# Two transformer layers on one core: the issue order of a list-scheduling planner, after key shifts drawn from a kept list of seeds

## The chip, the cores and the metric

The kernel runs on one core of a Trainium2 chip, as one launch. The core has five engines that each work through a queue of instructions in a fixed order: PE (matrix multiply), DVE (vector), ACT (scalar and activation functions), POOL (a second, slower vector engine) and SP, which here only issues transfers. An instruction starts when the one ahead of it on its engine lets it and when the data and buffers that it needs are there; semaphores carry this between engines. The metric is the device time of the launch in microseconds (us). Three runs of the kernel before took 1334.98, 1337.83 and 1337.9 us; the median is 1337.83 us.

## The reference

One batch of 1024 latent tokens (a grid of 16 rows by 64 columns) and 256 context tokens, both 1024 wide, goes through two layers. Layer A is grouped-query attention with 16 query heads on 4 key and value heads; layer B is neighbourhood attention with 16 heads, a window of 8 by 16 grid positions, a learned bias and the context tokens as extra keys. Each layer has its own modulation vectors, a gate branch and an output projection. What is computed, cut to its core:

```python
for i in range(2):
    sh_x, sc_x, g_x = split(silu(c) @ w_mod[i] + b_mod[i])        # and the same with c_ctx for the context
    hx = rms_norm(x, norm_g[i]) * (1 + sc_x) + sh_x
    hc = rms_norm(ctx, norm_g[i]) * (1 + sc_c) + sh_c
    # layer 0: q, k, v, z = hx @ w_in; q, k = rope(rms_norm(q)), rope(rms_norm(k)); keys and values of ctx go ahead
    #          p = softmax(q k^T / 8 over 1280 keys);  yx = ((p v) * silu(z)) @ w_out; the same for ctx with its own keys
    # layer 1: q, k, v, z = hx @ w_in;  p = softmax([q k_window^T / 8 + rpb, q k_ctx^T / 8])
    #          yx = ((p_window v_window + p_ctx v_ctx) * silu(z)) @ w_out
    x = x + g_x * yx
    # layer 0 alone: ctx = ctx + g_c * yc
return rms_norm(x, final_norm_g)
```

All of it is in 32-bit floats in the reference.

## The kernel before

**Precision.** Products run in 16-bit floats. An operand that needs more is split into a high part (a cast) and a low part (what the cast left over, times a power of two), and a product is then two or three matmuls. The splits are the work of ACT (casts), DVE and POOL (differences).

**Layer A** goes through the heads in pairs, eight of them. For each pair PE makes the projections (tile `pa`, line 1029), DVE, ACT and POOL norm and rotate them, and a pass of score products (`pm`, lines 1063 and 1069) gives the row maxima. Then come the score products themselves. Most heads use products that stand with keys on the partitions (`st`, lines 1255 and 1256); ACT takes two exponentials (`ph` in 16 bits, line 1240; `pf` in 32 bits, line 1242), POOL takes their difference (`pl`, line 1125, in two halves), and PE multiplies with the values (`pv`, lines 1131 to 1133). Some heads use products with queries on the partitions (`qs`, lines 1181 and 1182); their probabilities `qpp` are turned by a transfer (line 1200, a transpose that SP issues) before PE uses them (`qpv`, lines 1206 and 1208). The output projection of the layer is `poa` (line 1353), with a DVE product (`tm`, line 1357) and a POOL sum into `x` (line 1358) behind each tile. The modulation vectors of the second layer come from `pmg` (line 636), which reads weights `wg` that a transfer brings.

**Layer B** first norms `x` again (an ACT square at line 668 into `hrb`, DVE at 672 and 673, casts at 684), and makes its projections in a form with fewer products: sums of weight blocks `wtb` (POOL, lines 1429 to 1431, from loaded blocks `wsb`) are cast to `wb` (high part on ACT at line 1433, low part on DVE at 1434) and used at lines 1512 (`pwq`) and 1560 (`pwv`), with the context's products at 1522 (`pbc`) and 1572 (`pvc`). Attention then runs by head pair: scores `bsn` against the window and `bsc` against the context (lines 1593 and 1594), bias and row maximum on DVE (line 1612) with a bias table `tb` that POOL makes (lines 1412 to 1414), exponentials on ACT (1630 to 1633), the split on POOL (1125 again), a transposing transfer `bpht` (line 1636), and the products with the values (`bpv`, lines 1641 to 1644). The output weights `wsob` are loaded (line 1298), scaled (line 1300, POOL) and split (`wob`, line 726 on DVE); the output projection is `pob` (line 1734), then a sum and the last norm.

**What sets the order.** The Python code records all instructions once, with the stages interleaved by a coarse plan. Then class `Planner` reads them back: `graph` finds the dependencies and the buffers that each instruction opens, `cost` gives each an estimated time, and `schedule` plays the five engines forward. Each engine keeps a heap of the instructions whose inputs are there, and takes the one with the smallest key. `deadlines` works back from a finished schedule to a due time for each instruction. The key of a PE instruction is its start in the schedule before, and that of any other is its due time. `refine(5, …)` repeats this five times and keeps the order with the smallest modelled end. `apply` then fixes each engine's order by a dependency from every instruction to its next one. Names in the listings further down end in numbers that tell buffers and instances apart (`x19` is a tile of `x`, `poa00` the first output projection tile, `qpp1130` a probability tile).

Of the kernel before, what the change touches and what calls it, by code (L numbers as in the profile page):

```python
# [37 lines left out]
BEV, BLAG = 8, 4  # L38
BP0, BP1 = 0, 0.95
PFB, PHB, PTB = 5, 4, 6  # L40


class Planner:
# [437 lines left out]
        end = max(done)  # L481
        return [min(v, end) for v in due]

    def refine(self, rounds, margin, deadline):

        best = (max(self.done), self.order)
        self.log = [best[0]]
        for _ in range(rounds):
            due = self.deadlines(deadline)
            key = [s if e == "PE" else v for s, e, v in zip(self.start, self.eng, due)]  # L490
            best = min(best, (self.schedule(key.__getitem__, margin=margin), self.order), key=lambda b: b[0])
            self.log.append(max(self.done))
        self.order = best[1]

    def apply(self):
        info = mybir.DependencyInfo(mybir.DependencyClass.NoSync, mybir.DependencyReason.DATA)
# [1343 lines left out]
```

## Time and profile before

The profiled execution took 1334.24 us, 3.59 us under the median of the runs. Its span, from the first to the last record, is 1332.5 us; 1.74 us lie around it.

| what | value |
|---|---|
| runs, us | 1334.98, 1337.83, 1337.9 (median 1337.83) |
| profiled execution, us | 1334.24 (span 1332.5, mean clock of PE 0.995) |
| PE busy | 1300.4 us, 98% of the span, 14948 matmuls |
| DVE busy | 1071.4 us, 80% |
| ACT busy | 966.0 us, 72% |
| POOL busy | 888.1 us, 67% |
| idle time of PE | 32.1 us |
| chain that ended last | PE 74%, DVE 12%, ACT 6%, DMA 4%, issue 2%, POOL 1% |

The table's last row follows the work that ended last back to the start, at each step to what released it. In the views below, a row of a timeline gives the start and the length in us, the engine, the line of the code, the operation, the tile written and the tiles read, and at its end in brackets how long the engine stood idle ahead of it and which instruction released it. Ends of matmuls are modelled, so that each looks longer than its share of the engine: the starts tell the pace. A row of a table by stretch gives the stretch, its length, then for PE, weight loads, DVE, ACT and POOL the busy time with the number of instructions, and last the granted clock of PE, the share of the DMA engines and GB/s.

### The profile page before, as it was taken

The numbers are of one execution on the slowest core, as the hardware profiler recorded it, in microseconds if no ns is written. First come the engines' busy times: TensorE is split into PE (matmuls) and PEld (weight loads), VectorE is DVE, ScalarE is ACT, GpSimd is POOL, SyncE is SP. The second block draws the span as 40 slices with busy tenths as digits, with TensorE's granted clock in tenths as the row PEclk, the third lists the DMA queues.
The fourth block names the chain that finished last, engine by engine and source line by source line (L and its number), as shares of the span: only waits on it lengthen the run. The fifth ranks groups of instructions, "written<-read, shape, count | busy, mean of one in ns | idle before, by whom it ended". The sixth has DMA issues, their size and how long they took to land.

```text
span 1332.5 us, 38402 instructions
## 1 busy us (share of the span) xinstructions
PE 1300.4 (98%) x14948; PEld 923.5 (69%) x14948; DVE 1071.4 (80%) x2451; ACT 966.0 (72%) x2076; POOL 888.1 (67%) x1214
## 2 busy tenths in 40 slices
PE   9999999999999999999999989999999999999997
PEld 4457777777777777776654448779687786968553
DVE  5897787888889786769628997888888898989475
ACT  4653888878988877698742456878879788887453
POOL 2322777766877767687876456687766867877452
PEclk9999999999999999999999999999999999999999
DMA  9825467886777323244318962587766888979962
GB/s 368 245 69 121 96 136 140 158 158 137 150 150 143 69 67 83 59 123 105 102 36 211 224 144 81 120 155 152 154 135 148 149 146 149 169 159 208 294 150 107
DMA packets 391791, 192.17 MB, mean 144 GB/s; under 512 B 350072, under 2 KB 356408, under 8 KB 391608
## 3 DMA queue, kind: packets, MB, share of 16 engines
q1 hardware_dynamic: 391032, 189.67, 64.0%
q8 instruction: 117, 1.92, 0.6%
q14 instruction: 66, 0.54, 0.1%
q10 hardware_dynamic: 576, 0.03, 0.0%
HBM read 91.54 MB, written 15.75 MB: 81 GB/s over the span
## 4 chain that ended last, share of the span: by engine, by line
PE 74%; DVE 12%; ACT 6%; DMA 4%; issue 2%; POOL 1%; SPq 0%; DVEq 0%; POOLq 0%; ACTq 0%
PE pa L1029 13%; PE poa L1353 7%; PE pob L1734 6%; PE st L1256 3%; PE st L1255 3%; PE pm L1063 3%; PE pv L1132 2%; PE pv L1133 2%; PE pv L1131 2%; DVE wb L1434 1%; PE pkv L882 1%; DMA qpp<-qpp 1%; PE pbc L1522 1%; PE qpv L1206 1%; PE qs L1181 1%
## 5 line engine op out<-in xcount | busy, mean ns | idle before, releaser
L1125 POOL TENSOR_TENSOR pl<-pf,ph 128x256 f16<-128x256 f32 x400 | 271.7, 703 | 67.8 <-ACT pf L1242 44.0
L1125 POOL TENSOR_TENSOR bph<-bpf,bph 128x256 f16<-128x256 f32 (+1 forms) x224 | 184.8, 851 | 105.5 <-ACT bpf L1632 84.3
L1029 PE MATMUL pa<-wa,x 128*128 128x256 f16 x1536 | 226.0, 273 | 0.5 <-DVE mrow L638 0.4
L1240 ACT ACTIVATE ph<-st 128x512 f16<-128x512 f32 x240 | 144.2, 606 | 60.3 <-PE st L1256 56.9
L1560 PEld LDWEIGHTS <-hx 128*128 128x128 f16 x2688 | 157.6, 98 | 11.5 <-issue 3.6
L1029 PEld LDWEIGHTS <-x 128*128 128x128 f16 x1536 | 140.1, 98 | 35.0 <-issue 2.0
L1242 ACT ACTIVATE pf<-st 128x512 f32<-128x512 f32 x240 | 144.7, 608 | 1.7 <-DVE pl L1122 1.3
L1064 DVE TENSOR_REDUCE mxp<-pm 128x1 f32<-128x512 f32 x192 | 127.3, 685 | 16.3 <-PE pm L1063 14.2
L1131 PE MATMUL pv<-v,ph 128*128 128x65 f16 x960 | 126.0, 193 | 0.0
L1132 PE MATMUL pv<-v,ph 128*128 128x64 f16 x960 | 125.9, 195 | 0.0
L1125 POOL TENSOR_TENSOR qpp<-qpf,qpp 128x256 f16<-128x256 f32 (+1 forms) x158 | 92.9, 611 | 48.0 <-ACT qpf L1198 31.5
L1133 PE MATMUL pv<-v,pl 128*128 128x65 f16 x960 | 123.8, 192 | 0.0
L1512 PEld LDWEIGHTS <-wb 128*128 128x128 f16 x672 | 63.1, 98 | 69.3 <-issue 4.8
L1630 ACT ACTIVATE bph<-bpf,bnx 128x384 f16<-128x384 f32 (+1 forms) x128 | 70.6, 584 | 53.3 <-DVE bnx L1622 39.9
L1131 PEld LDWEIGHTS <-ph 128*128 128x128 f16 x960 | 91.1, 97 | 22.5 <-issue 0.2
L1132 PEld LDWEIGHTS <-ph 128*128 128x128 f16 x960 | 90.8, 97 | 15.3
L1133 PEld LDWEIGHTS <-pl 128*128 128x128 f16 x960 | 91.4, 99 | 11.3 <-POOL pl L1125 1.3
L1255 PE MATMUL st<-q,k 128*128 128x512 f16 x240 | 90.9, 379 | 1.4 <-ACT pf L1242 1.3
L1256 PE MATMUL st<-q,k 65*128 65x512 f16 x240 | 91.2, 383 | 0.0
L1353 PE MATMUL poa<-woa,oa 128*128 128x512 f16 x384 | 90.2, 379 | 0.0
L1734 PE MATMUL pob<-wob,obf 128*128 128x512 f16 x336 | 80.0, 379 | 0.0
L1429 POOL TENSOR_TENSOR wtb<-wsb 128x256 f32<-128x256 f32 x64 | 58.7, 918 | 31.9 <-DVE wb L1434 7.5
(480 smaller groups left out, 4035.4 us busy)
## 6 DMA issues: line engine op xcount, KB each, us to landing
wg<-in_w_mb SPq DMA_DIRECT2D x32, 512.0 KB
wsb<-in_b_wp SPq DMA_DIRECT2D x64, 256.0 KB
wm<-in_w_m SPq DMA_DIRECT2D x16, 512.0 KB
wsa<-in_a_wq SPq DMA_DIRECT2D x32, 256.0 KB
xstage<-in_x SPq DMA_DIRECT2D x8, 512.0 KB
wsoa<-in_a_w_out SPq DMA_DIRECT2D x16, 256.0 KB
x<-in_x SPq DMA_DIRECT2D x8, 512.0 KB
x_d<-x SPq DMA_DIRECT2D x8, 512.0 KB
```

What stands on the lines that cost most here:

```text
L1029: T.matmul(ps[:, :, i, :], hA(a, kt, t), wt[w][:, kt, :], start=n == 0, stop=n == 3 * KT - 1)
L1125: G.tensor_tensor(lo[:, c], p32[:, c], hi[:, c], op=ALU.subtract)
L1131: T.matmul(pv[:, t, :], hi[:, c], v[:, 0:65], start=first and t == 0, stop=False)
L1132: T.matmul(pv[:, t, 0:HD], hi[:, c], v[:, 65:129], start=False, stop=False)
L1133: T.matmul(pv[:, t, :], lo[:, c], v[:, 0:65], start=False, stop=last and t == n - 1)
L1240: S.activation(ph, st, AF.Exp)
L1242: S.activation(p32, st, AF.Exp)
L1255: T.matmul(so, k1[:, g, kc], q1[:, :, i, :], start=True, stop=False)
L1256: T.matmul(so, k2[0:65, g, kc], q2[0:65, :, i, :], start=False, stop=True)
L1353: T.matmul(ps, lhs(a, kt), w[b][:, kt, :], start=n == 0, stop=n == 3 * KT - 1)
L1560: T.matmul(ps[:, t * P:(t + 1) * P], hx[a][:, t, blk, kt], wt[j][:, s_, w, kt], start=first and t == 0 and m == 0, stop=last and t == 3 an ...
L1734: T.matmul(ps, ob[kt][:, t, a], wout["b"][hf][b][:, kt, :], start=n == 0, stop=n == 3 * len(kts) - 1)
```

## The change

`refine(5, …)` is replaced by `settle(2, seeds, …)`. Two rounds of due times and scheduling are run as before, without choosing among them. Then, for each of about 330 numbers in the kept list `NUDGE`, a random generator with that number as its seed draws a time between 0 and 1330 us, a width (2, 10 or 40 us), a spread (0.3, 1 or 4 us) and a subset of the five engines; the keys of the instructions of these engines that lie in that stretch of time are shifted by normal draws of that spread, one draw for each output tile on each engine. One last call of `schedule` with the shifted keys gives the order. The instructions, their operands and buffers stay as they were; so do the dependencies that `graph` finds, and only the order on each engine is another. Lines of the new kernel stand 37 further down than those of the kernel before (1353 is 1390).

```diff
+NUDGE = (
+    "688836 233264 233275 606456 325627 589506 889935 702195 564303 420536 171248 386454 369054 445142 567028 "
...
+)
...
-    def refine(self, rounds, margin, deadline):
-
-        best = (max(self.done), self.order)
-        self.log = [best[0]]
+    def settle(self, rounds, seeds, margin, deadline):
+
         for _ in range(rounds):
             due = self.deadlines(deadline)
             key = [s if e == "PE" else v for s, e, v in zip(self.start, self.eng, due)]
-            best = min(best, (self.schedule(key.__getitem__, margin=margin), self.order), key=lambda b: b[0])
-            self.log.append(max(self.done))
-        self.order = best[1]
+            self.schedule(key.__getitem__, margin=margin)
+        names = {}
+        group = np.array([names.setdefault(e + next((a.bass_ap.tensor.name for a in x.outs if hasattr(a, "bass_ap")), ""),
+                                           len(names)) for e, x in zip(self.eng, self.node)])
+        eng = np.array([("ACT", "DVE", "PE", "POOL", "SP").index(e) for e in self.eng])
+        key, free = np.array(key), np.ones(len(key), bool)
+        key[list(self.glued)], free[list(self.glued)] = -1.0, False
+        for seed in seeds:
+            r = np.random.default_rng(seed)
+            t0 = r.random() * 1330e3
+            width, spread = (2e3, 10e3, 40e3)[r.integers(3)], (300.0, 1000.0, 4000.0)[r.integers(3)]
+            on = r.random(5) < 0.5
+            sel = (key >= t0) & (key < t0 + width) & on[eng] & free
+            key[sel] += r.normal(0, spread, len(names))[group[sel]]
+        self.log = [self.schedule(key.tolist().__getitem__, margin=margin)]
...
-        plan.refine(5, 100.0, 200.0)
+        plan.settle(2, map(int, NUDGE.split()), 100.0, 200.0)
```

The order stays the same at large: an instruction moves by about 2 us of its engine's work (root mean square 2.0 us on PE, 2.7 on DVE, 2.2 on ACT, 1.8 on POOL, 1.7 on SP). Three places show how.

The first place is on SP, about 272 us into the span, in layer A. `wsa50` to `wsa53` are four weight loads of 256 KB each, `qpp1130` to `qpp1132` the probability tiles that are transposed, and `q122` is a transpose of queries. Before:

```order
L1200 DMA_TRANSPOSE qpp1122_4281<-qpp1122_4281 128x4x128
L1052 DMA q221_3706<-q121_3705 64x1024
L839 DMA wsa50_6883<-in_a_wq 128x512
L839 DMA wsa51_7064<-in_a_wq 128x512
L839 DMA wsa52_7232<-in_a_wq 128x512
L839 DMA wsa53_7411<-in_a_wq 128x512
L1200 DMA_TRANSPOSE qpp1130_4418<-qpp1130_4418 128x8x128
L1051 DMA_TRANSPOSE q122_4306<-q1624_4649 128x4x128
L1200 DMA_TRANSPOSE qpp1131_4435<-qpp1131_4435 128x8x128
```

And now:

```order
L876 DMA wsa50_6883<-in_a_wq 128x512
L876 DMA wsa51_7064<-in_a_wq 128x512
L1237 DMA_TRANSPOSE qpp1122_4281<-qpp1122_4281 128x4x128
L1088 DMA_TRANSPOSE q122_4306<-q1624_4649 128x4x128
L876 DMA wsa52_7232<-in_a_wq 128x512
L876 DMA wsa53_7411<-in_a_wq 128x512
L1237 DMA_TRANSPOSE qpp1130_4418<-qpp1130_4418 128x8x128
L1237 DMA_TRANSPOSE qpp1131_4435<-qpp1131_4435 128x8x128
```

Of the four loads two now stand ahead of the transpose of `qpp1122`, and two are left directly ahead of that of `qpp1130`; the transpose of `q122` has moved ahead of it. In the whole program 215 loads stood among the four rows ahead of a probability transpose, and 232 do now.

The second place is on PE, about 624 us into the span, where the last head of layer A (`st7000` to `st7009`) is scored, and the output projection `poa00` (inputs `oa0`, `oa1`, …) begins. Before, the rows up to the score product `st7003`:

```order
L1132 MATMUL pv612_12246<-v1_124,phc61_12252 128x64
L1133 LDWEIGHTS plc61_12256
L1133 MATMUL pv612_12246<-v1_124,plc61_12256 128x65
L1255 LDWEIGHTS k1_122
L1255 MATMUL st7003_12382<-q170_10822,k1_122 128x512
```

And now, at the place where `st7003` stood:

```order
L1390 MATMUL poa00_12832<-woa01_12693,oa0_2321 128x512
L1390 LDWEIGHTS oa0_2321
L1390 MATMUL poa00_12832<-woa00_12692,oa0_2321 128x512
L1100 LDWEIGHTS q171_11395
L1100 MATMUL pm73030_12237<-k1_122,q171_11395 128x512
```

Before, no `poa00` product stood ahead of `st7008`; now 13 of them stand between `st7002` and `st7007`, with row-maximum products `pm` beside them.

The third place is on POOL, about 775 us into the span, where layer B begins: the last sums into `x18` and `x19` meet the first weight sums. `wtb010` is a sum of weight blocks whose last part is line 1431 (now 1468), and `x19<-…tm91` the last sum into `x`. Before:

```order
L1429 TENSOR_TENSOR wtb010_14547<-wsb010_14546 128x256
L1358 TENSOR_TENSOR x19_14204<-x19_14204,tm90_14231 128x512
L1358 TENSOR_TENSOR x18_14128<-x18_14128,tm81_14259 128x512
L1430 TENSOR_TENSOR wtb010_14547<-wsb010_14546,wtb010_14547 128x128
L1358 TENSOR_TENSOR x19_14204<-x19_14204,tm91_14319 128x512
L1431 TENSOR_TENSOR wtb010_14547<-wsb010_14546,wtb010_14547 128x128
L1486 MEMSET bv10_14334 128x20
```

And now:

```order
L1466 TENSOR_TENSOR wtb010_14547<-wsb010_14546 128x256
L1395 TENSOR_TENSOR x19_14204<-x19_14204,tm90_14231 128x512
L1395 TENSOR_TENSOR x18_14128<-x18_14128,tm81_14259 128x512
L1467 TENSOR_TENSOR wtb010_14547<-wsb010_14546,wtb010_14547 128x128
L1523 MEMSET bv10_14334 128x20
L1468 TENSOR_TENSOR wtb010_14547<-wsb010_14546,wtb010_14547 128x128
L1395 TENSOR_TENSOR x19_14204<-x19_14204,tm91_14319 128x512
```

The last part of `wtb010` has gone ahead of the last sum into `x19`. On ACT, the rows that use these two results, before:

```order
L1452 COPY e1q0_14390<-pwq0a_14337 128x512
L668 ACTIVATE hrb80_14347,lssb8_14353<-x18_14128 128x1024
L668 ACTIVATE hrb90_14372,lssb9_14374<-x19_14204 128x1024
L1433 ACTIVATE wb011_14545<-wtb010_14547 128x4x128
L1433 ACTIVATE wb010_14544<-wsb011_14556 128x3x128
```

And now:

```order
L1489 COPY e1q0_14390<-pwq0a_14337 128x512
L705 ACTIVATE hrb80_14347,lssb8_14353<-x18_14128 128x1024
L1470 ACTIVATE wb011_14545<-wtb010_14547 128x4x128
L705 ACTIVATE hrb90_14372,lssb9_14374<-x19_14204 128x1024
L1470 ACTIVATE wb010_14544<-wsb011_14556 128x3x128
```

The cast of `wtb010` to `wb011` has gone ahead of the square of `x19`, in the same way.

22 rows, old and new, of the table NUDGE are left out of this document.

## The prediction

> **What bounds the kernel now.** I read the busy times first, then the table of stretches, the list of waits of PE, the chain of waits, and last the timelines at the places that the waits name. Each engine's busy time and its share of the span of 1332.5 us:
>
> ```profile
> PE 1300.4 (98%) x14948; PEld 923.5 (69%) x14948; DVE 1071.4 (80%) x2451; ACT 966.0 (72%) x2076; POOL 888.1 (67%) x1214
> ```
>
> PE is the bound: 1332.5 − 1300.4 = 32.1 us are all that it stands idle. The instructions stay the same, so a new order can win those 32 us at most, and some more that the busy time hides; it can lose without such a limit. Where the idle time lies, by stretches (the first four numbers: stretch, length, PE busy):
>
> ```profile
> 0.00:66.62 66.62, 61.32 (x398) 30.68 (x399) 48.11 (x124) 37.27 (x70) 19.46 (x29) 0.97 0.89 307
> 199.88:466.38 266.50, 261.45 (x3345) 201.06 (x3342) 223.21 (x611) 229.15 (x526) 201.22 (x309) 0.99 0.71 138
> 599.62:666.25 66.63, 64.56 (x829) 43.02 (x827) 51.57 (x105) 52.41 (x106) 53.32 (x74) 1.00 0.37 104
> 732.88:799.50 66.62, 60.78 (x332) 29.35 (x330) 63.73 (x97) 33.63 (x61) 33.40 (x35) 1.00 0.79 184
> 1199.25:1265.88 66.63, 64.78 (x745) 44.81 (x743) 46.85 (x108) 41.78 (x92) 40.96 (x45) 1.00 1.03 251
> 1265.88:1332.50 66.62, 59.11 (x421) 30.47 (x419) 41.12 (x86) 30.04 (x69) 28.90 (x31) 0.97 0.49 129
> 330.00:361.00 31.00, 30.90 (x408) 23.53 (x406) 27.23 (x79) 29.46 (x72) 25.62 (x39) 1.00 0.69 135
> ```
>
> The idle time of PE by them: 5.3 us at the front, 5.05 in the attention of layer A, 2.07 at its last head, 5.84 at the border of the layers, 1.85 where layer B's attention runs out, 7.5 at the end. The last row serves below. PE's waits by what released them:
>
> ```profile
> PE qpv L1206 <- DMA qpp<-qpp: 2.9, 3, 2.1
> PE pwv0c L1560 <- ACT wb L1433: 2.2, 1, 2.2
> PE pwv0c L1560 <- DVE wb L1434: 2.1, 2, 1.9
> PE bsn L1593 <- DVE bmx L1612: 1.9, 2, 1.0
> PE qs L1181 <- DVE qmx L1185: 1.5, 3, 0.6
> ...
> PE st L1255 <- ACT pf L1242: 1.3, 2, 1.0
> PE pm L600 <- DMA wm<-in_w_m: 1.2, 2, 0.6
> ...
> PE pmg L636 <- DVE q L817: 0.2, 1, 0.2
> ```
>
> (us in all, times, longest; 25 rows with 35 waits, of which the last stands at the end.) No wait is long. The new order helps where it puts other work of PE into such a gap, or brings the releaser forward, and hurts where it opens a new gap.
>
> **The change part by part.**
>
> *A, the border of the layers.* The timeline there, first of PE:
>
> ```profile
> 779.76 0.22 PE L1560 MATMUL pwv0c<-wb,hx 128*128 128x128 f16 x1 [2.20 <-ACT wb L1433]
> ```
>
> of POOL:
>
> ```profile
> 776.30 1.71 POOL L1358 TENSOR_TENSOR x<-x,tm 128x512 f32<-128x512 f32 x1
> 777.97 0.90 POOL L1431 TENSOR_TENSOR wtb<-wsb,wtb 128x128 f32<-128x128 f32 x1
> ```
>
> and of ACT:
>
> ```profile
> 778.04 1.06 ACT L668 ACTIVATE hrb<-x 128x1024 f16<-128x1024 f32 x1 [1.38 <-POOL x L1358]
> 779.00 0.19 ACT L668 ACTIVATION_READ_ACCUMULATOR hrb<-x 128x1 f32 x1
> 779.10 0.61 ACT L1433 ACTIVATE wb<-wtb 128x512 f16<-128x512 f32 x1
> ```
>
> PE waits 2.20 us for a cast on ACT (779.10), which stands behind a square (778.04), which waits for POOL's sum into `x` (1.71 us); the weight sum that the cast needs comes after that sum. In the new order both the weight sum and the cast go ahead. The weight sum can then end 1.71 us earlier. The sum into `x` ends 0.90 us later, and the square and the norm behind it move by as much; DVE is full in that stretch (63.73 of 66.62 us), so part of this comes back in the later waits for DVE's `wb`. Between 1.71 and 1.71 − 0.90 = 0.81 I take the middle: **1.3 us**. Bounds: 0 (all given back) and 5.84, the stretch's whole idle time.
>
> *B, the end of layer B's attention.* The first wait on PE:
>
> ```profile
> 1222.74 0.27 PE L1594 MATMUL bsc<-bk,bq 128*128 128x256 f16 x1
> 1223.99 0.32 PE L1593 MATMUL bsn<-bk,bq 128*128 128x384 f16 x1 [0.97 <-DVE bmx L1612]
> ```
>
> DVE at the same time:
>
> ```profile
> 1222.52 1.06 DVE L726 SCALAR_TENSOR_TENSOR wob<-wsob,wob 128x512 f16<-128x512 f32 x1
> 1223.51 0.41 DVE L1612 CUSTOM_DVE_ANT_1 bpf<-bsn,tb 128x256 f32<-128x256 f32 x1
> ```
>
> The second wait, DVE and then PE:
>
> ```profile
> 1232.70 0.42 DVE L1612 CUSTOM_DVE_ANT_1 bpf<-bsn,tb 128x256 f32<-128x256 f32 x1 [1.77 <-POOL tb L1414]
> ```
>
> ```profile
> 1233.19 0.34 PE L1593 MATMUL bsn<-bk,bq 128*128 128x384 f16 x1 [0.88 <-DVE bmx L1612]
> ```
>
> The third score product of a head needs the buffer that DVE's line 1612 clears of the first, and that instruction stood behind a weight split of 1.06 us. Now it stands ahead of this split, and 22 products of `pvc` stand between the first and the second score product. The 0.97 us go. At the second wait DVE itself is late by the bias table; in the new order PE has about 3.6 us more work between the first and the third product there, against 0.88 us. Both go: **1.85 us**, bounds 0 (the table comes later by as much) and 1.85.
>
> *C, the last head of layer A.* The wait, and the long run of output products behind it in the chain of waits:
>
> ```profile
> 625.24 0.38 PE L1255 MATMUL st<-q,k 128*128 128x512 f16 x1 [1.04 <-ACT pf L1242]
> ```
>
> ```profile
> 695.60 64.33 PE poa L1353 x298
> ```
>
> A score product waits until ACT has cleared a score buffer. The new order puts four products of `poa` and two of `pm` between this product and the one before it; a `poa` product takes 64.33 / 298 = 0.216 us, so four and the two alike make 1.3 us against 1.04. They come out of the run at 695.60, in which PE waits for nothing, so they cost nothing where they leave. The weights' transfer for `pmg` is issued two rows earlier on SP, and `pmg` follows earlier too. I take **2.0** of the stretch's 2.07 us; as low bound 0.5, since `poa` now needs its weights' casts earlier, on an ACT that is 52.41 of 66.63 us busy there.
>
> *D and E, transposed probabilities in layer A.* The chain of waits shows three transposes up to the products that they hold, PE the worst wait, SP the queue at that place, and the DMA queues carry:
>
> ```profile
> 201.73 4.24 DMA qpp<-qpp
> 273.68 7.15 DMA qpp<-qpp
> 411.31 5.03 DMA qpp<-qpp
> ```
>
> ```profile
> 280.88 0.29 PE L1206 MATMUL qpv<-v,qpp 128*128 128x128 f16 x1 [2.14 <-DMA qpp<-qpp]
> ```
>
> ```profile
> 271.50 2.01 SPq L839 DMA_DIRECT2D wsa<-in_a_wq  x4
> 273.68 1.25 SPq L1200 DMA_TRANSPOSE qpp<-qpp  x1
> 275.02 1.40 SPq L1051 DMA_TRANSPOSE q<-q  x1
> ```
>
> The slowest of the three stands right behind four loads. I put the difference to the fastest on them: (7.15 − 4.24) / 4 = 0.73 us for a load of 256 KB, an estimate. In the new order two loads are left directly ahead of it (2 × 0.73 = 1.46 us gained), and the transpose of `q` of 1.40 us has moved ahead of it (lost). PE has 1.77 us more work of its own ahead of the product. Net 1.8 of 2.14, and about half of it, **1.0**, since three transposes without a common cause differ by 2.9 us; bounds 0 and 2.14. E is the rest of that stretch, 5.05 − 2.14 = 2.9 us in waits of 0.3 to 0.8 us. A third, **1.0**, bounds 0 and 2.9.
>
> *F, the front.* Loads change places there; PE's waits for such a load sum to 1.2 us in the list. The rows of the first 12 us don't change. **0**, bounds −1.2 and 1.2.
>
> *G, new waits.* At 330 to 361 us PE stands idle 0.10 us. There, the transposes of `qpp` in the new order have 4.2 to 5.4 us between POOL's result and PE's use, while the chain's rows above needed 4.24 to 7.15, 5.03 in the middle: 5.03 − 4.2 = 0.8, so **−1.0**, bounds 0 and −2.9 (7.15 − 4.24).
>
> *H, what the busy time hides.* At B the starts are 1223.99 − 1222.74 = 1.25 us apart, where its like starts 0.11 us behind; the row shows 0.97 of the 1.14 lost. So a wait hides 0.17 us. Some eight waits go: **1.4**, bounds 0 and 6.0 (0.17 for each of 35 waits in the list).
>
> *The end.* The last piece of the chain is as it was, the same matmuls in the same order behind it:
>
> ```profile
> 1301.03 23.97 PE pob L1734 x111
> ```
>
> So what PE gains before carries through. Sum: 1.3 + 1.85 + 2.0 + 1.0 + 1.0 − 1.0 + 1.4 = 7.55 us. Against the profiled execution 1334.24 − 7.55 = 1326.7; the median of the runs lies 3.59 above it, so **1330.3 us**. With every term at its low end the sum is −3.4 (1341.2), with every term at its high end 22 (1316).
>
> **The rivals.**
>
> *L, a larger gain.* D and E come whole and each of the 35 waits loses its hidden part: 7.55 + 1.1 + 1.9 + 4.6 = 15.2 us, **1322.7**. For it: the hidden part is in every wait that I looked at. Against it: order alone must remove nearly all waits of layer A, with DVE at 223 and ACT at 229 of 266.5 us. [...]
>
> *N, waits swapped.* The gains at A to E are matched by new gaps of the same size, since neither DVE nor ACT gets faster: an instruction moved by 2 us meets waits of 0.3 to 2 us. The sum is 0, **1337.8**. For it: DVE's full stretch at A. Against it: B and C have their cover in rows.
>
> *S, slower: transposes land later.* Of the loads, 232 instead of 215 stand among the four rows ahead of a probability transpose. At 0.73 us each the 17 more cost up to 12.4 us, if all reach PE. Loads and transposes are issued by the same queue (the rows at 271.50 and 273.68). Then 7.55 is more than used up: 1330.3 + 12.4 = **1342.7**. It decides from 11.5 us on, that is, if nearly all of the 17 delays reach PE. Without D's and E's gain, which hang on the same transposes, it is 1344.7, and 9.5 us decide. For it: `qpp` heads the list of waits. Against it: only 3 of 96 such transposes make PE wait now, and loads ahead of a transpose that has slack cost nothing. [...]
>
> **How the numbers follow.** A measurement of this kernel tells a difference of about 0.3%, 4.0 us, from none: faster is under 1333.8, slower over 1341.8. The forecast gets 0.54 (its own range 1326 to 1336, with 0.07 of it over 1333.8), L 0.12, N 0.14, S and other new waits of its kind 0.20. Faster: 0.47 + 0.12 = 0.59; same: 0.07 + 0.14 = 0.21; slower: 0.20. The range from 1321 to 1344 takes in L and most of S, and leaves out some 0.15.
>
> **What would show it.** In the new trace: at the border PE's wait for ACT's `wb` under 1.2 us (A); no wait of `bsn` for line 1649 after 1215 us (B); the stretch around 600 to 666 us with under 0.3 us idle and `poa` products beside `st` (C); the wait of `qpv` at about 280 us under 1.2 us (D); the idle time of PE at 24 to 26 us instead of 32.1. Wrong would be: waits of `qpv` or `bpv` for transposes over 6 us in all (S), or idle time that has moved to other lines at the same sum (N).

## The result, and the profile after

The changed kernel took 1323.66 us (median of 4 runs, 1322.63 to 1324.77); the kernel before stands at 1336.4 us over four runs. The ratio is 0.9908 with a 95% interval of 0.9888 to 0.9928, so 10 to 15 us faster; a second set of runs, told of below, gave 1321.45 us and 0.9893 (0.9871 to 0.9914). The forecast was 1330.3 us, which is 7.5 us under the median of the three runs that it started from and 6.1 us under that of the four; the medians differ by 12.7. So it fell on the right side, with about half of the size. The profiled execution of the changed kernel took 1324.77 us with a span of 1322.9, 9.6 us shorter than the one before.

The page's busy times after the change:

```profile
PE 1296.9 (98%) x14948; PEld 920.0 (70%) x14948; DVE 1064.1 (80%) x2451; ACT 963.5 (73%) x2076; POOL 891.3 (67%) x1214
```

PE stands idle 1322.9 − 1296.9 = 26.0 us instead of 32.1. That is 6.1 us of the 9.6. The other 3.5 us are busy time of PE, 1300.4 down to 1296.9, for the same 14948 matmuls. The table by stretches, at the places of the prediction (the columns are those of before; the third number from the end is PE's granted clock):

```profile
0.00:66.15 66.15, 60.24 (x386) 29.68 (x387) 50.05 (x119) 35.40 (x67) 19.78 (x29) 1.00 0.88 297
197.00:461.00 264.00, 262.77 (x3369) 202.37 (x3367) 228.33 (x622) 230.19 (x532) 204.93 (x311) 1.00 0.74 143
595.00:661.00 66.00, 65.25 (x832) 42.88 (x831) 49.11 (x100) 51.75 (x105) 52.01 (x74) 1.00 0.38 105
727.00:794.00 67.00, 62.86 (x374) 32.00 (x372) 61.85 (x97) 33.38 (x60) 36.58 (x38) 1.00 0.79 183
1124.00:1190.60 66.60, 64.77 (x881) 50.67 (x880) 57.28 (x134) 54.94 (x119) 49.68 (x64) 1.00 0.85 157
1190.60:1257.00 66.40, 66.40 (x770) 46.52 (x768) 43.00 (x104) 41.15 (x88) 39.61 (x45) 1.00 1.02 239
1257.00:1322.90 65.90, 58.02 (x416) 29.91 (x413) 39.44 (x84) 31.49 (x73) 29.11 (x31) 0.96 0.51 138
```

The attention of layer A has 1.2 us of idle time where 5.05 stood. Its last head has 0.75 (was 2.07), the border of the layers 4.1 (was 5.84), the end of layer B's attention none (was 1.85). One stretch got worse: 1.8 us at 1124 to 1190 us. The waits of PE, the longest and the one at the border:

```profile
PE pkv L919 <- ACT x L913: 2.3, 2, 1.3
PE pwq7b L1549 <- DVE bk L1541: 1.6, 1, 1.6
PE idle L873 <- DVE zero L590: 1.5, 1, 1.5
PE pwq0b L1549 <- DVE w2q L1501: 1.4, 1, 1.4
PE pm L1100 <- ACT q L853: 1.2, 1, 1.2
PE pwv0c L1597 <- ACT wb L1470: 1.2, 2, 1.0
PE qpv L1243 <- DMA qpp<-qpp: 0.9, 1, 0.9
```

The wait of `qpv` for transposes, which headed the list with 2.9 us, is down to 0.9 (1.5 in a second profile, below); `bsn` has gone from the list. The last piece of the chain of waits is nearly the one of before:

```profile
1290.42 24.62 PE pob L1771 x114
```

**The clock.** Before, the clock fell to half at three places within the work of PE. One of them is the place D of the prediction:

```profile
280.00:281.00 1.00, 0.12 (x2) 0.13 (x3) 0.00 (x0) 0.35 (x1) 1.00 (x2) 0.92 0.53 113
281.00:282.00 1.00, 1.00 (x17) 1.00 (x17) 0.00 (x0) 0.26 (x1) 0.11 (x1) 0.50 1.29 274
282.00:283.00 1.00, 1.00 (x9) 0.69 (x7) 0.00 (x0) 1.00 (x3) 0.00 (x0) 0.50 0.14 32
283.00:284.00 1.00, 1.00 (x4) 0.45 (x3) 0.76 (x2) 0.16 (x2) 0.76 (x2) 0.50 0.20 50
284.00:285.00 1.00, 1.00 (x10) 0.81 (x9) 0.69 (x3) 0.00 (x0) 0.54 (x1) 0.87 0.00 0
```

The 0.08, 0.50, 0.50, 0.50 and 0.13 us that these rows lose make 1.71 us, so half clock for 3.4 us. The same 1.71 us are lost at 14 to 19 us and at 127 to 131 us. In the profile after, no stretch has a clock under 1.00 until PE has finished. That most of the 3.5 us of busy time go with the clock, and not with PE's order, is seen in one of the experiments below. It leaves PE's order as it was before and moves rows of SP alone; its profile has no half clock within the work either, and PE is busy almost as short as after the change:

```profile
PE 1297.4 (97%) x14948; PEld 921.3 (69%) x14948; DVE 1069.8 (80%) x2451; ACT 966.6 (72%) x2076; POOL 891.0 (67%) x1214
```

### The profile page after: what moved, and what is told of

Same layout as the page of the kernel before. It is cut to its first block, busy times and chain, and to the rows that moved or that the text cites. A ratio compares the mean times of both kernels' runs of the same rounds, so it can differ in the third digit from the quotient of the medians.

```text
span 1322.9 us, 38359 instructions
## 1 busy us (share of the span) xinstructions
PE 1296.9 (98%) x14948; PEld 920.0 (70%) x14948; DVE 1064.1 (80%) x2451; ACT 963.5 (73%) x2076; POOL 891.3 (67%) x1214
## 4 chain that ended last, share of the span: by engine, by line
PE 60%; DVE 7%; POOL 3%; ACT 2%; issue 2%; DMA 1%; POOLq 0%; DVEq 0%; ACTq 0%
PE pa L1066 7%; PE pob L1771 6%; PE poa L1390 4%; PE st L1292 3%; PE st L1293 3%; PE pm L1100 2%; PE pv L1169 2%; PE pv L1170 2%; PE pv L1168 2%; PE pvc L1609 1%; PE pbc L1559 1%; PE bpv L1680 1%; PE bsn L1631 1%; PE bsn L1630 1%; PE bpv L1681 1%
## 5 line engine op out<-in xcount | busy, mean ns | idle before, releaser
L1162 POOL TENSOR_TENSOR bph<-bpf,bph 128x256 f16<-128x256 f32 (+1 forms) x224 | 189.5, 867 | 93.0 <-ACT bpf L1669 73.5
L1066 PE MATMUL pa<-wa,x 128*128 128x256 f16 x1536 | 231.3, 272 | 0.3 <-DVE q L854 0.3
L1277 ACT ACTIVATE ph<-st 128x512 f16<-128x512 f32 x240 | 141.3, 600 | 58.2 <-PE st L1293 52.4
L1597 PEld LDWEIGHTS <-hx 128*128 128x128 f16 x2688 | 163.0, 98 | 8.9 <-issue 1.9
L1101 DVE TENSOR_REDUCE mxp<-pm 128x1 f32<-128x512 f32 x192 | 128.1, 683 | 14.1 <-PE pm L1100 12.5
L1169 PE MATMUL pv<-v,ph 128*128 128x64 f16 x960 | 130.9, 195 | 0.0
L1168 PE MATMUL pv<-v,ph 128*128 128x65 f16 x960 | 130.4, 193 | 0.0
L1170 PE MATMUL pv<-v,pl 128*128 128x65 f16 x960 | 128.7, 192 | 0.0
L1466 POOL TENSOR_TENSOR wtb<-wsb 128x256 f32<-128x256 f32 x64 | 53.5, 837 | 42.5 <-DMA wsb<-in_b_wp 28.4
```

Source lines behind the costliest of these rows:

```text
L1066: T.matmul(ps[:, :, i, :], hA(a, kt, t), wt[w][:, kt, :], start=n == 0, stop=n == 3 * KT - 1)
L1162: G.tensor_tensor(lo[:, c], p32[:, c], hi[:, c], op=ALU.subtract)
L1168: T.matmul(pv[:, t, :], hi[:, c], v[:, 0:65], start=first and t == 0, stop=False)
L1169: T.matmul(pv[:, t, 0:HD], hi[:, c], v[:, 65:129], start=False, stop=False)
L1170: T.matmul(pv[:, t, :], lo[:, c], v[:, 0:65], start=False, stop=last and t == n - 1)
L1277: S.activation(ph, st, AF.Exp)
```

## The experiments

One measure is used throughout. For each matmul, take the time from its start to the next start and subtract the median of its kind (tile and shape) in the profile before. For two kinds that start in bursts (`pm` from `wm`, and `pmg`) the mean stands in for the median; with the median the sums below would both be 22.4 us higher. The sum over a stretch is called its late starts. It holds waits, their hidden part, and the loss at half clock. It is 40.0 us before and 30.0 after.

Most experiments mix the two orders. Both are computed in one kernel; the instructions up to a named product of PE come in one order, those up to a second in the other, and so on:

```diff
+    def weave(self, plans, pieces):
+        ...
+        put, order = set(), {e: [] for e in self.order}
+        for which, upto in pieces:
+            o, start = plans[which]
+            cut = 1e18
+            if upto:
+                cut = min(start[i] for i in o["PE"] if out[i].split("_")[0] == upto)
+            for e, l in o.items():
+                order[e] += [i for i in l if i not in put and start[i] < cut]
+            for e in o:
+                put.update(order[e])
+        self.order = order
...
         plan.schedule(margin=100.0)
+        plan.refine(5, 100.0, 200.0)
+        old = plan.order, plan.start
+        plan.schedule(margin=100.0)
         plan.settle(2, map(int, NUDGE.split()), 100.0, 200.0)
+        plan.weave({"B": old, "A": (plan.order, plan.start)}, PIECES)
```

**Four parts of the program, each alone in the new order.** The theory was that the gain sits where PE's late starts shrink and that the places add up; the rival was that the order works only as a whole.

```diff
+PIECES = (("A", "st1003"), ("B", None))                       # p_first
+PIECES = (("B", "st1003"), ("A", "st4116"), ("B", None))      # p_second
+PIECES = (("B", "st4116"), ("A", "bsn000"), ("B", None))      # p_third
+PIECES = (("B", "bsn000"), ("A", None))                       # p_fourth
```

> The new order up to the first product of tile st1003 (197.6 us into the span before), the old order of the instructions that are left from there on. Summing how much later each matmul starts than its kind usually does gives 40.0 us before and 30.0 us after for the whole program. In this part it is 14.4 before and 14.5 after. Theory that the gain lies where PE's late starts shrink: no difference here, within 1.5 us. Rival, that the order works only as a whole: the seam costs something, 2 to 5 us slower than before.

> The new order from st1003 to st4116 (197.6 to 466.7 us), the old one ahead and behind. Late starts in this part: 10.3 us before, 4.1 after, of which some 1.6 us come from the matmuls that run at half clock behind the 2.14 us wait at 280.88. First theory: about 6.2 us faster than before. If the half clock there is an accident of that one profile: about 4.6. Rival, order as a whole: under 2 us.

> The new order from st4116 to bsn000 (466.7 to 806 us), the old one ahead and behind. Late starts: 12.2 us before, 8.3 after. First theory: about 3.9 us faster. The prediction's terms A and C alone: 3.3. Rival, order as a whole: under 1.5 us.

> The old order up to bsn000, the new one from there to the end. Late starts: 3.1 us before and after, since the 2.2 us gained at the prediction's place B come back as a new wait of about as much at 1165 to 1171 us. First theory: no difference, within 1 us. The prediction's term B alone: 1.85 us faster.

The kernel before took 1335.91 us beside them (31 runs).

| part | median, us | ratio (95%) | us from the ratio |
|---|---|---|---|
| first, to 198 us | 1334.32 | 0.9988 (0.9973 to 1.0003) | −1.6 |
| second, 198 to 467 us | 1330.28 | 0.9957 (0.9942 to 0.9973) | −5.7 |
| third, 467 to 806 us | 1332.56 | 0.9973 (0.9957 to 0.9989) | −3.6 |
| fourth, 806 us to the end | 1332.98 | 0.9983 (0.9970 to 0.9995) | −2.3 |

The four sum to −13.2 us; the whole gave −12.3 and −14.3 by its two ratios. So the parts add up, within intervals of about 2 us to each side for each of them, and the rival falls. The second and third came out as expected. The first holds no gain that can be told from none. The fourth was expected at zero and gained 2.3. Its profile says why. The gain at place B is there as expected, while the new wait behind it, 1.6 us in the profile of the changed kernel, is short in this execution. PE's waits from 1125 to 1240 us in that run:

```profile
PE pwq7b L1577 <- DVE bk L1569: 0.4, 1, 0.4
```

These four, the two profiles before and after and the repeat below give several executions of each order for each place. Late starts in us, by stretches of 66.6 us or sums of them (the old order's executions, then the new one's):

| stretch | old order | new order | difference of the means |
|---|---|---|---|
| 0 to 200 us (F) | 14.4, 14.6, 16.1, 12.9 | 14.6, 14.1, 16.2 | +0.5 |
| 200 to 466 (D, E, G) | 10.3, 11.9, 9.9, 12.2 | 4.1, 5.0, 5.2 | −6.3 |
| 600 to 666 (C) | 3.4, 3.8, 2.7, 3.4 | 2.0, 1.4, 1.1 | −1.8 |
| 733 to 866 (A) | 7.5, 7.7, 7.6, 6.9 | 5.3, 4.8, 6.5 | −1.9 |
| 1132 to 1199 | 0.3, 0.2, 0.2, 0.3 | 2.4, 1.3, 0.7 | +1.2 |
| 1199 to 1266 (B) | 2.2, 2.0, 2.3, 2.0 | −0.1, −0.1, −0.1 | −2.2 |

In the first stretch the executions of one order differ by up to 3 us.

**The changed kernel once more, for the clock.** No edit.

> The changed kernel once more, beside the kernel before on the same chip, for its clock over more executions. If a part of the gain is half clock that no longer falls: the mean clock over the runs at 0.9975 to 0.9985 against 0.995 before, which is (0.0025 to 0.0035) x 1330 = 3.3 to 4.7 us of the gain, and two profiles that differ by that beyond their idle time. If the first four runs were luck: a clock of 0.9955 or less, and the gain from idle time alone, 6 to 9 us. In both cases the time is 1322 to 1327 us.

It took 1321.45 us (6 runs), the kernel before 1335.77 (11 runs). The mean clock was 0.9978, with 0.998 in the first four runs; the kernel before had 0.9951 over all its 77 executions beside these experiments. So the first theory holds: the clock differs by 0.0027. The time lies a little under the 1322 us that both theories gave. Over the 77 executions of the kernel before the time falls by 0.94 us for each 0.001 of clock (correlation −0.62). By that slope the clock would stand for 2.5 us of the gain; at its full value, 0.0027 × 1330, for 3.6. Both are estimates: a correlation doesn't show what the clock costs. The 3.5 us of busy time between the first two profiles are of that size. This run's profile has no half clock within the work either.

But this changes from one execution to the next. In the first 200 us, three of five profiles with the new order there do have half clock (that of the first part, and those of the two runs below that change the new order at one later place). At place D three of the five profiles with the old order on all engines have it, and none of the five with the new one. At the border of the layers it is three of seven with the old order and none of five with the new one; but there it cost nothing that can be seen, since the late starts from 733 to 866 us are 6.9 to 7.9 us in the three and 7.1 to 7.7 in the other four. The waits of PE from 195 to 466 us in the repeat:

```profile
PE qpv L1243 <- DMA qpp<-qpp: 1.5, 3, 1.0
PE qs L1218 <- DVE qmx L1222: 0.2, 1, 0.2
```

**Place D alone.** First all engines in the new order from 256 to 289 us, then SP alone, then the mirror image in the changed kernel.

```diff
+PIECES = (("B", "st2000"), ("A", "st2009"), ("B", None))      # d_all; in d_sp only SP's part of the middle piece
+PIECES = (("A", "st2000"), ("B", "st2009"), ("A", None))      # d_undone
```

> The order before, with the new order on all engines between st2000 and st2009 (256 to 289 us). PE's late starts there are 5.1 us in the profiled execution before: 1.2 in two waits of qs and of pa, 2.3 in the wait of qpv, 1.6 at half clock behind it. If the place stands alone and all of it goes: 3.4 us faster where the half clock didn't fall there, 5.1 where it did. The prediction's D (1.0) with its share of E (0.4): 1.4 us faster.

> The order before, with the new order on SP alone between st2000 and st2009 (256 to 289 us): two of the four loads ahead of the transpose of qpp1130 move ahead of another one, and the transpose of q122 moves ahead of it. If the loads make that transpose late, as the prediction's D has it (0.73 us each, less up to 1.4 for q122): PE's wait at about 281 us falls from 2.1 to 0.6 to 2.0 us, and the time by 0.1 to 1.5 us, by up to 1.6 more where the half clock behind it goes too. Rival, that PE's own order makes the difference: the wait stays at 2 us and the time within 1 us of before.

> The new order, with the old one on all engines between st2000 and st2009 (256 to 289 us before). The mirror image of the run that put the new order there alone and gained 3.3 us (0.9975). If the place stands alone: 3 to 5 us slower than the new kernel, 1327 to 1329 us, with PE's wait of qpv near 281 us back at 2 us. Rival, order as a whole: no wait there, since PE, SP and POOL come to the place otherwise spaced; under 1.5 us slower.

With all engines: 1334.38 us, ratio 0.9975 (0.9961 to 0.9989), 3.3 us faster. Undone in the changed kernel: 1325.45 against 1321.45 us, 4.0 slower, as expected (the time itself is under the 1327 written down, since the changed kernel was faster in this set). So this stretch of 33 us holds about a quarter to a third of the whole gain. The clock is a different matter: with all engines in the new order the mean clock is 0.9951, against 0.9950 for the kernel before beside it, so that gain came without the clock; with the place undone it falls from 0.9978 to 0.9965. With SP alone: 1338.52 us, ratio 1.0013 (0.9998 to 1.0028), so no gain and rather a loss. PE's longest waits from 255 to 290 us, with all engines:

```profile
PE pmg L701 <- DVE q L882: 1.0, 1, 1.0
PE qpv L1271 <- DMA qpp<-qpp: 0.7, 1, 0.7
```

from 260 to 290 us with SP alone:

```profile
PE st L1321 <- DMA q<-q: 2.9, 1, 2.9
PE qpv L1271 <- DMA qpp<-qpp: 2.7, 1, 2.7
```

and from 255 us on in the run that undoes it, with the clock behind the wait (278 to 283 us):

```profile
PE qpv L1271 <- DMA qpp<-qpp: 1.7, 1, 1.7
```

```profile
278.00:279.00 1.00, 0.66 (x12) 0.33 (x9) 0.00 (x0) 0.95 (x2) 0.20 (x1) 0.92 0.59 125
279.00:280.00 1.00, 1.00 (x5) 0.59 (x4) 0.54 (x1) 0.48 (x2) 0.44 (x1) 0.50 0.65 145
280.00:281.00 1.00, 1.00 (x5) 0.51 (x4) 0.48 (x3) 0.00 (x0) 0.85 (x2) 0.50 0.27 66
281.00:282.00 1.00, 1.00 (x7) 0.67 (x6) 1.00 (x5) 0.00 (x0) 0.00 (x0) 0.50 0.00 0
282.00:283.00 1.00, 1.00 (x14) 0.72 (x13) 0.25 (x1) 0.63 (x2) 0.00 (x0) 0.87 0.00 0
```

With SP alone, two loads fewer and the transpose of `q122` more stand ahead of the transpose, and the wait is 2.7 us. The chain of waits shows why, from the issue of the transpose to the product that it holds, first with SP alone, then with all engines (7.15 us before):

```profile
278.90 5.75 DMA qpp<-qpp
284.70 0.23 PE L1271 MATMUL qpv<-v,qpp 128*128 128x128 f16 x1 [2.68 <-DMA qpp<-qpp]
```

```profile
274.76 6.36 DMA qpp<-qpp
281.16 0.23 PE L1271 MATMUL qpv<-v,qpp 128*128 128x128 f16 x1 [0.70 <-DMA qpp<-qpp]
```

So from issue to product the transpose took 1.40 us less with SP alone. But PE arrived at 284.70 − 2.68 = 282.02, only 3.1 us behind the issue, where it was 5.1 us before (280.88 − 2.14 − 273.68). SP came later to the issue. The transpose of `q` now stands ahead of it, and SP stood still for 1.4 us before that one (274.95 to 276.32), waiting for a result of DVE:

```profile
273.73 1.22 SPq L1265 DMA_TRANSPOSE qpp<-qpp  x1
276.32 1.19 SPq L1116 DMA_TRANSPOSE q<-q  x1
277.56 1.23 SPq L904 DMA_DIRECT2D wsa<-in_a_wq  x2
```

With all engines, it took 0.79 us less from issue to product, and PE arrived 5.7 us behind the issue; the two make the 1.44 us that the wait fell by. There SP doesn't stand still ahead of the transpose of `q`. So in both runs the time from issue to product is shorter with SP's new rows (5.75 and 6.36 us against 7.15), and only with the new order on the other engines does SP come in time. What the loads alone do is left open: in the run with the new order in the third part, four loads stand ahead of the transpose as before, and it took 5.7 us at most. PE's order alone wasn't tried. With the old order put back, wait and half clock both came back.

**The wait filled, for the clock alone.** In the kernel before, one product just ahead of the wait at 280.88 us is repeated 16 times into the same place; the order is otherwise as before.

```diff
                 for j in range(2):
-                    T.matmul(pm[:, j, :], q1[:, t0 + j, i, :], k1[:, g, NX * P:TOK], start=True, stop=True)
+                    for _ in range(1 + FILL.get((u, b, i, j), 0)):
+                        T.matmul(pm[:, j, :], q1[:, t0 + j, i, :], k1[:, g, NX * P:TOK], start=True, stop=True)
+FILL = {(2, 3, 0, 0): 16}
```

> The kernel before with 16 repeats of one product (tile pmc230, 128x256, 0.108 us each, 1.73 us in all) just ahead of the 2.14 us wait of qpv at 280.88; they write the same numbers to the same place again, and the rest of the order is as before. PE does more work, and waits less. If the half clock behind that wait comes from PE standing still: no half clock at 281 to 285 us in the profile, the mean clock over the runs up by 0.0005 to 0.0013, the time 0 to 1.6 us lower. If the wait alone counts: the same time as before, within 0.7 us, and the half clock still there in some of the executions. If the repeats push the work behind them: up to 1.7 us slower.

The repeats stand in the timeline as one group with their two originals, and the wait behind them is short:

```profile
279.57 2.13 PE L1081 MATMUL pmc<-k,q 128*128 128x256 f16 x18
```

```profile
282.53 0.23 PE L1218 MATMUL qpv<-v,qpp 128*128 128x128 f16 x1 [0.49 <-DMA qpp<-qpp]
```

The clock behind it stays up:

```profile
282.00:283.00 1.00, 0.51 (x14) 0.47 (x13) 0.82 (x3) 1.00 (x3) 0.00 (x0) 1.00 0.94 197
283.00:284.00 1.00, 1.00 (x17) 0.82 (x14) 0.23 (x1) 1.00 (x3) 0.88 (x2) 1.00 0.90 196
```

The time was 1335.22 us, ratio 0.9993 (0.9980 to 1.0006): 1.7 us of matmuls were added at no cost that can be told from none. The mean clock was 0.9946 over 12 executions, against 0.9950 for the kernel before. So the profile agrees with the clock theory at this place, and the mean clock, which should have risen by 0.0005 to 0.0013, does not. A single profile without half clock says little here, since two of those with the old order and the wait left unfilled have none either (third and fourth part). The run is inconclusive on what the half clock costs.

**No draws.** The list of seeds is left empty.

```diff
-        plan.settle(2, map(int, NUDGE.split()), 100.0, 200.0)
+        plan.settle(2, (), 100.0, 200.0)
```

> The new kernel with an empty list of seeds: two rounds of due times and scheduling, no shifts, and no choice among rounds. If the shifts bring the gain: 1333 to 1340 us, like before. Rival, that it came with giving up refine's choice of the modelled best: under 1328 us, like the new kernel.

1340.83 us, ratio 1.0028 (1.0012 to 1.0045), just over the expected range, and far from the rival. Two rounds without choosing lose 3.7 us, and the shifts bring these and 12 to 14 us more. The waits at the head of the list are longer than before:

```profile
PE qpv L1243 <- DMA qpp<-qpp: 5.0, 5, 2.3
PE pwv0c L1597 <- DVE wb L1471: 2.7, 2, 2.5
```

**The one new wait taken out.** The changed kernel with the old order from 1122 to 1193 us.

```diff
+PIECES = (("A", "bsn511"), ("B", "pwv7a"), ("A", None))       # mended
```

> The new order, with the old one between bsn511 and pwv7a (1122 to 1193 us before), where the new order has late starts of 2.4 us in its profile (a wait of 1.61 us of pwq7b for a cast on DVE) and the old one 0.2. If that wait is the order's: 1 to 2 us faster than the new kernel, no wait of pwq7b over 0.5 us. Rival: the wait is an accident of that execution, as the run with the new order from bsn000 on suggests, where it was 0.4 us; then no difference, within 0.7 us.

1322.75 us, ratio 0.9906 (0.9880 to 0.9931): no faster than the changed kernel beside it (1321.45), so neither expectation came out. The wait of `pwq7b` is gone and another stands at the seam, with half clock behind it (0.50 at 1190 to 1192 us):

```profile
PE pwv7b L1625 <- DVE c12q L1542: 2.2, 1, 2.2
```

No kernel here beats the changed one.

## Why the prediction was right in direction and short in size

The bound was read rightly: PE is the bound, and only its late starts could be won. The step that failed is the size of D and E, the waits for transposed probabilities and those beside them. The terms, against the table of stretches:

- **A, 1.3 us forecast, 1.9 measured.** Right. The cast that PE waits for came earlier: the wait for ACT's `wb` fell from 2.20 us to 1.0. Part of it came back on DVE, as said, but in a wait of 1.4 us of `pwq0b` for `w2q`, where the prediction named the waits for `wb`; these fell from 2.1 to 0.7 us.
- **B, 1.85 forecast, 2.2 measured.** Right, in every execution.
- **C, 2.0 forecast, 1.8 measured.** Right in size, and the `poa` products stand beside `st`. But 0.75 us of idle time are left in that stretch, where the prediction asked for under 0.3.
- **D and E, 2.0 forecast, 1.0 with G's loss taken off; 6.3 measured, with G's loss in it.** This is the step that failed, as a size. D was bounded by its wait of 2.14 us and then halved, E was put at a third. Both went for the most part: of 5.05 us of idle time 1.2 are left. Three things were missed. The first: in that profile, 1.6 us of late starts at half clock stood behind the wait of D; the quoted row by stretch showed the clock as 0.99 and I passed over it. Not every execution has them, and place D alone gained its 3.3 us without a better mean clock. The second: one execution undersells these waits. In the profile before, the `qpv` product near 206 us starts 0.7 us late; in the profiles of the third and the fourth part, which have the old order there, it is 2.2 and 2.4. The third: E's waits of `qs`, `pa` and `pv` are not random. They are four late starts of 0.5 to 0.7 us that stand in each execution of the old order and in none of the new.
- **D's working was sounder than the halving.** It gave 1.8 us before it was halved; with all engines at that place the wait fell by 1.44. Its 0.73 us for a load ahead of a transpose was an estimate from three rows, and stays one: with two loads fewer and one transpose more the time from issue to product was 0.8 and 1.4 us shorter, but in one execution with all four loads it was as short. What the working left out is that the row moved ahead on SP can itself wait for its data: in the run with SP alone it held up what stands behind it by 1.4 us.
- **F, 0 forecast, +0.5 measured,** within the spread of that stretch. Right as a sum. The waits for the loads fell from 1.2 us to 0.4, while those of `pkv` for ACT rose from 1.0 to 2.3.
- **G, a new wait of 1.0 us.** Right on place and size in some executions: `qpv` starts 1.2 us late at 340 us in the repeat, but not in the first profile. A second new wait, 1.2 us in the mean at 1132 to 1199 us, was not foreseen.
- **H, 1.4 us of hidden time, 3.5 us of busy time measured.** The term looked for the part of a wait that the rows conceal. Nine waits fewer are in the list (26 instead of 35), near the eight that it counted. What it lacked is the clock: PE's busy time differs by 3.0 us between the profile before, with half clock at three places, and the run with SP alone, with none (1300.4 and 1297.4 us), and PE's order is the same in both. It is not a separate sum: the late starts of D and E hold a part of it.

The low end of the prediction's sum has a slip: its terms make −3.6 us, not −3.4.

The terms as measured sum to −6.3 − 1.8 − 1.9 − 2.2 + 1.2 + 0.5 = −10.5 us, with the rest of the program near zero; the two profiles differ by 10.0. The medians differ by 12.7: the profiled execution before lay 2.2 us under its median (1334.24 against 1336.4), the one after 1.1 over its own. The 14.3 of the repeat lie within the intervals.

**The rivals.** L gave 1322.7 and lay nearest. Its first half, that D and E come whole, is what happened for the most part. Its second, that each of the 35 waits loses its hidden 0.17 us, is not: 26 waits are left. That it lay so near is in part luck. N is refuted by the table: only one stretch took a wait in exchange. S is refuted by the time, and by the waits of `qpv`, which fell though more loads stand ahead of such transposes. Its price was also too high from the start. By the same count in the rows of SP, only 7 of the 17 loads stand ahead of the 96 transposes of `qpp` that the prediction names; the other 10 are in layer B, ahead of transposes into `bpht`, for which PE waits in neither profile.

## What to carry to other kernels

Where an order alone changes and one engine is busy 98%, cost each place from its waits, and then look at the clock behind them: in the profile before, 1.6 us of late starts at half clock stood behind the wait of 2.14 us, while at the border of the layers the late starts were 6.9 to 7.9 us with half clock and 7.1 to 7.7 without. The wait for a transfer varied here from execution to execution (the same `qpv` near 206 us started 0.7, 2.2 and 2.4 us late), so a single profile gave its order of size and no more, while the waits of PE for other engines at place B came to 2.0 to 2.3 us of late starts in all four executions, and could be counted whole. The gains of four separate parts added up here (13.2 us against 12.3 and 14.3 for the whole), so a prediction that summed them needed no discount for the sum, only for each. And a transfer that is moved ahead in a queue can bring a wait of its own, in which the queue stands still, as SP did for 1.4 us ahead of the transpose of `q`.

## What the runs showed of the hardware that I had not expected

- PE's clock halved for 3.4 us at a time, losing 1.71 us (twice as long and as much in some profiles), within a kernel whose PE is 98% busy. It did so behind a single wait of 2.14 us (280.88) and behind a run of waits none of which is over 0.75 us (123 to 127 us). It did not behind the wait of 2.20 us at 779.76, though it did behind that same wait, at 2.0 to 2.3 us, in three other profiles with the old order there. It did not behind the waits of 2.9 and 2.7 us of the run with SP alone. Nor did it in the changed kernel at 125 to 129 us, where PE stood idle 1.8 of 4 us, against 2.06 us at 123 to 127 before:

```profile
125.00:126.00 1.00, 0.38 (x4) 0.18 (x3) 1.00 (x5) 0.78 (x2) 0.00 (x0) 1.00 0.00 0
126.00:127.00 1.00, 0.25 (x3) 0.02 (x1) 1.00 (x3) 0.95 (x4) 0.00 (x0) 1.00 0.00 0
```

  In the run of the first part, and in the one with the new wait taken out, the same waits stand there and the clock did halve behind them (mean clock 0.994 in both profiled executions, against 0.998). So the same waits had half clock behind them in some executions and not in others, and the length of the wait alone doesn't tell the two apart: half clock stood behind 2.14 us in the profile before, none behind 2.9 and 2.7 us. What sets it is not shown.
- The kernel before spread over 1331.5 to 1342.9 us in its 77 executions beside the experiments, the changed one over 1320.8 to 1324.8 in its 10, with the same instructions. With the slope of 0.94 us for each 0.001 of clock, a part of that spread goes with the clock; that the half clock is its cause isn't shown.
